# Plain 32-bit products for the cache compression of a hybrid decoder step, state scaling inside the update, and stationary keys in the prompt's compressed scores

## The chip, the cores and the metric

One Trainium2 chip, one of its cores. The metric is device time of one execution in microseconds (us), the median over runs; for the kernel before it is 1252.94 us (three runs, 1251.83 to 1259.93). TensorE multiplies, VectorE (DVE), ScalarE (ACT) and GpSimd (POOL) do the elementwise work, SyncE (SP) issues most transfers.

## The reference, cut to what matters

One layer on a prompt of 512 tokens and on 8 sample sequences of 4 new tokens with 2048 cached ones. The part that the change touches: the compression of cached keys and values (k and v alike, 8 sequences, 2 heads of 64), the compressed scores of the prompt, and the state update of the sample's mLSTM.

```python
def compress(kv, pe, w1, b1, w2):            # once for keys, once for values
    b, tk, hk, dh = kv.shape
    nc = tk // CMP_STRIDE                    # 16 rows a block
    half = CMP_STRIDE * dh                   # 1024
    ch = kv.reshape(b, nc, CMP_STRIDE, hk, dh).transpose(0, 1, 3, 2, 4).reshape(b, nc, hk, half)
    first = ch @ w1[:half]
    second = ch @ w1[half:]                  # w1: 2048 x 256
    second = jnp.concatenate([second[:, 1:], jnp.zeros_like(second[:, :1])], axis=1)
    hid = first + second + (pe.reshape(-1) @ w1 + b1)
    return jax.nn.gelu(hid) @ w2
...
        s_c = jnp.einsum('bkgqd,bkcd->bkgqc', qi, kc) - slopes * d_c     # compressed scores
...
        C_new = w_c[..., None, None] * C + jnp.einsum('bsh,bshe,bshd->bhed', w_s, vi, ki)
```

Everything is float32 in and out.

## The kernel before

The kernel is written with a tile framework whose scheduler simulates the program and so sets the order on each engine; pools of buffers and data dependencies bound it. Work runs in stages: projections and the prompt's selected and window attention (0 to about 240 us), then compression with everything else of the two attentions beside it (to 573 us), the rest of the sample's attention (to 647 us), then output projection, cross attention and feed-forward.

Dense products run as three fp32r matmuls. `split` (L213, L214) makes a high part by a ScalarE copy into fp32r and a low part by a subtraction on VectorE or GpSimd; `mm3` (L218 to L220) adds high by high, high by low and low by high into one PSUM bank.

`compress(kv)` is a generator, for keys (0) and values (1): 32 steps each, (b, t) with b one of 8 sequences and t one of 4 quarters of w1. For a step, `produce` (two steps ahead) fetches gathered pages (`cgat`, indirect transfers on GpSimd's queue, L573), transposes them with VectorE into `xf` (L1193), lets GpSimd add the two halves (L1195), and splits `xf` into `xh` and `xl` (128x768 each, L1196). Then come six products, three pairs: half one, half two and the sum of the halves by the matching weights (the last by w0 + w1, so that three products stand for four), stationary x 128x128, moving weights 128x256. For b = 0 four more with `xe`, the prompt's own blocks and the position terms (66 rows). `weights(t)` splits a quarter of w1 into `w1h` and `w1l`, adds its halves on GpSimd (L1135) and splits the sum into `wsh` and `wsl`. At t = 3 `ys` is formed (L1328 to L1330) with `nxt_`, rows shifted by a transfer from `cur` (L1300 to L1302); one sequence later it is turned (L1216), goes through gelu and the second product (L1244, L1246).

w1 for the keys is staged in two buffers of the page pool and in `vcn`, `po2` and `r3`; for the values it is loaded into a pool "w1r" once the prompt's mLSTM is done.

`weave(compress(kv), fg)` runs the compression as background and takes steps of the foreground chain for credit: 0.6 for each compression yield (three a step). The chain is `front` (the prompt's mLSTM with `cmp_prompt`, the prompt's compressed attention, mixed in), `mlstm_s` (the sample's mLSTM), `sample` (its compressed, window and selected attention in two groups of four sequences) and `open_late`. `sample` starts only when the values' weights are split (`need(("w", 1))`, L1413). In `sample` pages are gathered into `gat` (L573), turned on TensorE (`keys`, L1512), scored four sequences at a time (`quad`, L1522), normalised with exp (L1667) and multiplied by values (L1688).

`mlstm_s` turns the old state `C0` (8 sequences, 4 heads, 128x128), reads it out, scales it by `wcb` on GpSimd (L1070, two instructions of 128x2048), and adds outer products (L1100) with VectorE (`outer`, L1101, eight of 128x512).

`cmp_prompt` scores 512 prompt tokens against 32 compressed keys: for each of four token tiles eight products with the queries stationary (128x128) and 32 key columns moving (L1359), and two additions of a bias (L1362).

## Time and profile before

| | |
|---|---|
| median of three runs | 1252.94 us (1251.83 to 1259.93) |
| profiled execution | 1257.88 us |
| its span | 1256.2 us |
| busy TensorE / VectorE / ScalarE / GpSimd | 94 / 69 / 50 / 46 % |
| mean granted TensorE clock | 0.97 |
| chain that ended last | TensorE 72%, VectorE 12%, issue 5%, DMA 3%, ScalarE 3%, GpSimd 2% |
| moved | HBM read 141.67 MB, written 13.12 MB |

The profile shows one execution. A line of the trace names the engine (PE is TensorE's matmuls, PEld its weight loads), the source line, the operation and the tiles (out<-in, numbers left out). A busy engine is one with an instruction in work; matmuls are pipelined and their ends are modelled, so their spacing is read from starts. PEclk is the clock granted to TensorE as a share of full speed (2.4 GHz; the lower level is 1.2). The chain of waits follows the work that ended last back in time, from each instruction to what released it.

### The profile page before, as it was taken

How to read it: one execution, taken by the hardware profiler on the slowest of the kernel's cores; microseconds unless marked ns; L12 is line 12 of the kernel's file. 1: busy time of each engine (PE TensorE's matmuls, PEld its weight loads, DVE VectorE, ACT ScalarE, POOL GpSimd, SP SyncE). 2: the span in 40 equal slices, each digit the busy share in tenths (PEclk: the TensorE clock that was granted, in tenths of full speed). 3: DMA queues.
4: the chain of work that ended last, by engine and by line, in shares of the span. 5: the costliest groups of instructions: out<-in, count | busy, mean ns of one | idle time of the engine just before them, and what ended most of it. 6: DMA issues, size and time to landing. Idle time of an engine off the chain costs nothing.

```text
span 1256.2 us, 24868 instructions
## 1 busy us (share of the span) xinstructions
PE 1174.9 (94%) x9388; PEld 1078.2 (86%) x9388; DVE 867.2 (69%) x1881; ACT 628.6 (50%) x1424; POOL 583.9 (46%) x696
## 2 busy tenths in 40 slices
PE   7999999889998779998989998999999999999996
PEld 5998999588986677876889987589899999999996
DVE  6336674577886876776556576544988878888874
ACT  5235666755546525567533333433565555465452
POOL 1013354577664854744234100034786486486443
PEclk9999999899888899999989999999999999999998
DMA  7324240132142464567659399750023322422411
GB/s 231 100 53 105 83 151 3 52 115 76 59 133 92 124 212 147 174 208 236 160 156 179 101 217 280 258 168 1 1 92 108 104 93 79 133 93 77 135 52 72
DMA packets 141771, 154.33 MB, mean 123 GB/s; under 512 B 17449, under 2 KB 123689, under 8 KB 141394
## 3 DMA queue, kind: packets, MB, share of 16 engines
q1 hardware_dynamic: 131922, 119.17, 31.9%
q0 software_dynamic: 9728, 33.56, 8.3%
q8 instruction: 74, 1.21, 0.4%
q14 instruction: 47, 0.39, 0.1%
HBM read 141.67 MB, written 13.12 MB: 123 GB/s over the span
## 4 chain that ended last, share of the span: by engine, by line
PE 72%; DVE 12%; issue 5%; DMA 3%; ACT 3%; POOL 2%; SPq 2%; another core or an unknown queue 0%; DVEq 0%; POOLq 0%; ACTq 0%
PE bd L218 7%; PE bd L220 7%; PE xc L2255 7%; PE xa L2255 7%; PE bd L219 6%; PE bd L2255 5%; PE tp L2255 5%; PE xa L219 2%; PE xa L218 2%; PE xa L220 2%; DVE sp L2195 2%; PE tp L634 1%; PE xc L219 1%; PE xc L218 1%; PE xc L220 1%
## 5 line engine op out<-in xcount | busy, mean ns | idle before, releaser
L214 POOL TENSOR_TENSOR al<-fraw,ah 128x512 fp32r<-128x512 f32 (+1 forms) x104 | 127.3, 1226 | 152.7 <-ACT ah L213 124.2
L214 DVE TENSOR_TENSOR wlo<-wraw,whi 128x1024 fp32r<-128x1024 f32 (+3 forms) x74 | 76.4, 1061 | 27.6 <-ACT whi L213 27.4
L213 ACT ACTIVATE whi<-wraw 128x1024 fp32r<-128x1024 f32 (+3 forms) x74 | 62.9, 890 | 64.7 <-DMA wraw<-in_w_xv 28.8
L218 PE MATMUL bd<-w1h,xh 128*128 128x256 f32 x256 | 78.8, 309 | 6.6 <-ACT xh L213 5.1
L213 ACT ACTIVATE ah<-fraw 128x512 fp32r<-128x512 f32 (+1 forms) x112 | 65.8, 593 | 37.8 <-PE xc L2255 11.7
L220 PE MATMUL bd<-w1h,xl 128*128 128x256 f32 x256 | 78.7, 313 | 6.3 <-DVE xl L214 6.3
L213 ACT ACTIVATE xh<-xf 128x768 fp32r<-128x768 f32 x64 | 53.5, 842 | 52.6 <-POOL xf L1195 30.7
L1195 POOL TENSOR_TENSOR xf<-xf 128x256 f32<-128x256 f32 x64 | 52.9, 834 | 56.6 <-DVE xf L1193 38.0
L219 PE MATMUL bd<-w1l,xh 128*128 128x256 f32 x256 | 76.1, 298 | 0.0
L214 DVE TENSOR_TENSOR xl<-xf,xh 128x768 fp32r<-128x768 f32 x64 | 62.9, 987 | 15.1 <-ACT xh L213 13.7
L625 POOL TENSOR_SCALAR sb<-sb,rs,gat 128x128 f32<-128x128 f32 (+3 forms) x64 | 45.9, 722 | 54.3 <-DVE rs L624 40.2
L218 PEld LDWEIGHTS bd<-w1h,xh 128*128 128x128 f32 x256 | 51.9, 203 | 11.2 <-ACT xh L213 7.1
L213 ACT ACTIVATE ah<-sp 128x512 fp32r<-128x512 f32 (+1 forms) x64 | 35.5, 555 | 50.3 <-DVE sp L2195 26.6
L220 PEld LDWEIGHTS bd<-w1h,xl 128*128 128x128 f32 x256 | 51.2, 202 | 10.6 <-DVE xl L214 7.6
L219 PEld LDWEIGHTS bd<-w1l,xh 128*128 128x128 f32 x256 | 52.0, 203 | 1.4 <-issue 0.9
L219 PE MATMUL bd<-hlo,whi 128*128 128x272 f32 x176 | 52.0, 296 | 0.0
L218 PE MATMUL bd<-hhi,whi 128*128 128x272 f32 x176 | 51.7, 294 | 0.0
L220 PE MATMUL bd<-hhi,wlo 128*128 128x272 f32 x176 | 51.4, 292 | 0.0
L2195 DVE TENSOR_TENSOR sp<-fraw 128x512 f32<-128x512 f32 (+1 forms) x32 | 47.9, 1497 | 0.2
L214 DVE TENSOR_TENSOR al<-sp,ah 128x512 fp32r<-128x512 f32 (+1 forms) x64 | 40.8, 637 | 9.7 <-ACT ah L213 8.5
L1869 POOL TENSOR_TENSOR acc<-acc,sq 128x272 f32<-128x272 f32 x35 | 31.3, 895 | 34.3 <-ACT sq L1868 33.9
L220 PE MATMUL bd<-hh,wlo 128*128 128x272 f32 x160 | 46.6, 292 | 0.0
(998 smaller groups left out, 4830.4 us busy)
## 6 DMA issues: line engine op xcount, KB each, us to landing
fraw<-in_w_gate SPq DMA_DIRECT2D x11, 1024.0 KB
fraw<-in_w_up SPq DMA_DIRECT2D x11, 1024.0 KB
fraw<-in_w_down SPq DMA_DIRECT2D x24, 384.0 KB
mkv<-in_cache_mem_k SPq DMA_DIRECT2D x64, 128.0 KB
mkv<-in_cache_mem_v SPq DMA_DIRECT2D x16, 512.0 KB
wraw<-in_w_in SPq DMA_DIRECT2D x8, 512.0 KB
wraw<-in_w_xq SPq DMA_DIRECT2D x4, 1024.0 KB
wraw<-in_w_xk SPq DMA_DIRECT2D x4, 1024.0 KB
```

The lines of the kernel that those rows point to most:

```text
L213: nc.scalar.activation(hi, src, AF.Copy)
L214: (eng or nc.gpsimd).tensor_tensor(lo, src, hi, op=OP.subtract)
L218: nc.tensor.matmul(out, ah, bh, start=first, stop=False, **kw)
L219: nc.tensor.matmul(out, ah, bl, start=False, stop=False, **kw)
L220: nc.tensor.matmul(out, al, bh, start=False, stop=last, **kw)
L625: (nc.vector, nc.gpsimd)[1].tensor_scalar(sb[:, :n], sb[:, :n], rs, gat[:, i, 3 * h + 1 + br:3 * h + 2 + br], op0=OP.mult, op1=OP.mult)
L634: ins = nc.tensor.transpose(p[:, 128 * k:128 * k + 128], sb[:, 128 * k:128 * k + 128], ident)
L1195: nc.gpsimd.tensor_tensor(xf[:, :, 128:192], xf[:, :, 0:64], xf[:, :, 64:128], op=OP.add)
L1869: nc.gpsimd.tensor_tensor(acc[hf], acc[hf], sq, op=OP.add)
L2195: nc.vector.tensor_tensor(o, a, b, op=op)
L2255: nc.tensor.matmul(p[:, :HALF], w[a][:, k], x[b_][:, k], start=first and k == 0 and i == 0, stop=last and k == n - 1 and i == 2, skip_grou ...
```

## The change

Three parts, and what they bring along.

1. Compression multiplies plain 32-bit operands: one `mm1` takes the place of each `mm3`. The splits of x, of the weights and of `xe` go. `weights(t)` is one VectorE addition. VectorE's transpose writes `xf` in the order that the products read, in four buffers instead of two; to make that possible the gathers take rows in another order (index tables at the start of the kernel), and so do the eviction in `hidden` and the shifted rows (two transfers of 64 and 63 rows instead of 112 and 15). w1 for the keys is loaded ahead into a pool "cx"; w1 for the values into tiles of the compression's own pool; "w1r" and the wait at the start of `sample` go.
2. `mlstm_s`: the GpSimd scaling goes; the update is 32 VectorE instructions C = C * wcb + p of 128x128.
3. `cmp_prompt`: keys are stationary (128x32), the 512 queries move, four products fill one bank in strips of 32 partitions; the result is copied to SBUF (`ST`), turned per token tile by two transposes, and one addition takes the place of two.

```diff
@@ gather tables
-            nc.gpsimd.iota(psel4[:, q], pattern=[[0, 4], [1, 8], [0, 4]], base=8 * (q % 2), channel_multiplier=-1,
+            nc.gpsimd.iota(psel4[:, q], pattern=[[0, 4], [1, 16], [0, 2]], base=0, channel_multiplier=-1,
...
+        cx = push("cx", side="left")
+        w1p = {}
+        for t in range(4):
+            w1p[0, t] = cx.tile([128, 2, 2, 256], F32, name=f"w1{t}"), cx.tile([128, 2, 256], F32, name=f"ws{t}")
+            load_w1(0, t, [w1p[0, t][0][:, s] for s in range(2)])
@@ mlstm_s
-                if c == 2 or c == 4:
-                    cc = C0[c // 2 - 1]
-                    b0 = 2 * c - 4
-                    nc.gpsimd.tensor_tensor(cc, cc, wcb[:, b0:b0 + 4, :, None].to_broadcast([128, 4, 4, 128]), op=OP.mult)
...
                     nc.tensor.matmul(p, W3[:, h], kz[:, 4 * c:4 * c + 4], start=True, stop=True)
-                    nc.vector.tensor_tensor(C0[c][:, :, h], C0[c][:, :, h], p.rearrange("p (b d) -> p b d", b=4), op=OP.add)
+                    for b in range(4):
+                        x = C0[c][:, b, h]
+                        nc.vector.scalar_tensor_tensor(x, x, wcb[:, 4 * c + b, h:h + 1], p[:, 128 * b:128 * b + 128],
+                                                       op0=OP.mult, op1=OP.add)
@@ compress
-            def weights(t, raw):
-                hi, lo = [cw.tile([128, 2, 2, 256], R32, name=f"w1{c}{t}") for c in "hl"]
...
-                nc.gpsimd.tensor_tensor(raw[0], raw[0], raw[1], op=OP.add)
-                split(sh, sl, raw[0], (nc.vector, nc.gpsimd)[1])
-                w1s.append(((hi[:, 1], lo[:, 1]), (hi[:, 0], lo[:, 0]), (sh, sl)))
+            def weights(t):
+                w, ws = w1p[kv, t]
+                nc.vector.tensor_tensor(ws, w[:, 0], w[:, 1], op=OP.add)
+                w1s.append((w[:, 1], w[:, 0], ws))
+
+            def mm1(out, a, b, first, last, **kw):
+                nc.tensor.matmul(out, a, b, start=first, stop=last, **kw)
...
+                if kv == 0 and b > 0 and t == 0 and b < 5:
+                    w1p[1, b - 1] = (cw.tile([128, 2, 2, 256], F32, name=f"w1{b - 1}"),
+                                     cw.tile([128, 2, 256], F32, name=f"ws{b - 1}"))
+                    load_w1(1, b - 1, [w1p[1, b - 1][0][:, s] for s in range(2)])
...
-                xf = cw.tile([128, 4, 192], F32, name="xf", bufs=2)
-                nc.vector.transpose(xf[:, :, 0:128].rearrange("p a (q i) -> p q a i", q=4),
-                                    gs[0].rearrange("p (q t a i) -> p t q a i", q=4, t=4, a=4)[:, t])
-                nc.gpsimd.tensor_tensor(xf[:, :, 128:192], xf[:, :, 0:64], xf[:, :, 64:128], op=OP.add)
-                xh, xl = [cw.tile([128, 2, 3, 128], R32, name=f"x{c}", bufs=2) for c in "hl"]
-                split(*[x.rearrange("p c g (v j) -> p v c g j", v=2) for x in (xh, xl)],
-                      xf.rearrange("p (v c) (g j) -> p v c g j", v=2, g=3), nc.vector)
+                xf = cw.tile([128, 2, 3, 128], F32, name="xf", bufs=4)
+                nc.vector.transpose(xf[:, :, 0:2].rearrange("p c g (x v i) -> p (g x) v c i", x=2, v=2),
+                                    gs[0].rearrange("p (q t v c i) -> p t q v c i", q=4, t=4, v=2, c=2)[:, t])
+                nc.gpsimd.tensor_tensor(xf[:, :, 2], xf[:, :, 0], xf[:, :, 1], op=OP.add)
...
-                        mm3(dst[i_], (ah[:, kk], al[:, kk]), (wh[:, kk], wl[:, kk]), i_ != 1 and t == 0 and kk == 0,
+                        mm1(dst[i_], ops[i_][:, kk], w1s[t][i_][:, kk], i_ != 1 and t == 0 and kk == 0,
                             t == 3 and kk == 1, skip_group_check=True)
...
-                            mm3(px[:66, 0:256], (eh[:, kk, sl], el[:, kk, sl]), (wh[:, kk], wl[:, kk]),
+                            mm1(px[:66, 0:256], xe[:, kk, s:s + 66], w1s[t][1 - s][:, kk],
@@ cmp_prompt
+            ST = vcn.rearrange("p (v c) o -> p v (c o)", v=2)
+            for v in range(2):
+                S = bank(psp)
+                for j in range(4):
+                    nc.tensor.matmul(S[32 * j:32 * j + 32], kb[:, v], Q2[:, 4 * v + j].bitcast(F32), start=True, stop=True)
+                nc.scalar.activation(ST[:, v], S, AF.Copy)
...
-                            nc.tensor.matmul(S[:, c0:c0 + 32], Q2[:, 4 * v + j, 128 * i:128 * i + 128].bitcast(F32), kb[:, v],
-                                             start=True, stop=True)
...
+                        nc.tensor.transpose(S[:, 128 * v:128 * v + 128], ST[:, v, 128 * i:128 * i + 128], ident)
+                    nc.vector.tensor_tensor(sb, S[:, :256].rearrange("p (h s) -> p h s", h=8), CB[:, i], op=OP.add)
@@ sample
-            yield from need(("w", 1))
```

The order on TensorE where compression begins (tp, sp and po rows are the prompt's mLSTM; bd and xa are the banks of the compression, w1h, w1l, wsh the split weights and their sum, xh and xl the split input). Before:

```order
L799 MATMUL tp<-xc,wqk 128x512
L825 MATMUL sp<-qm,kmT 128x384
L802 MATMUL tp<-xc,wqk 128x32
L218 MATMUL bd<-w1h_3342,xh 128x256
L219 MATMUL bd<-w1l_3343,xh 128x256
L218 MATMUL xa<-wsh_3346,xh 128x256
L218 MATMUL bd<-w1h_3342,xeh 66x256
```

The same place of the changed kernel (w and ws are the loaded weights and their sum, xf the transposed input):

```order
L822 MATMUL sp<-qm,kmT 128x384
L796 MATMUL tp<-xc,wqk 128x512
L799 MATMUL tp<-xc,wqk 128x32
L1128 MATMUL bd<-w_3200,xf 128x256 x4
L1128 MATMUL bd<-w_3206,xf 128x256 x4
L1128 MATMUL xa<-ws_3201,xf 128x256 x2
L1128 MATMUL bd<-w_3212,xf 128x256
```

The first eight products now need loaded weights and the transposed input alone; the first that needs a sum is the ninth.

The order on TensorE at the end of compression (gat the sample's gathered pages, kt its turned keys, PTs its turned probabilities, ys and hid the compression's last output, mh and ml the input of the output projection). Before:

```order
L220 MATMUL bd<-w1h_5524,xl 128x256
L1512 MATMUL tp<-ident,gat 128x128 x12
L1216 MATMUL xc<-ident,ys 128x128 x4
L1619 MATMUL tp<-ident,pcs 127x128
L1622 MATMUL tp<-blk,GS 128x32
L1522 MATMUL sp<-kt,Qn 32x512 x4
L1512 MATMUL tp<-ident,gat 128x128 x12
L1246 MATMUL xc<-w_5414,hid 127x64 x4
L1512 MATMUL tp<-ident,gat 128x128 x12
L1522 MATMUL sp<-kt,Qn 32x512 x4
L1512 MATMUL tp<-ident,gat 128x128 x12
L218 MATMUL xa<-mh,whi 128x272
```

And in the changed kernel (L1482, L1492 and L1658 are the key transposes, scores and value products, L1364 the prompt's compressed output):

```order
L1128 MATMUL bd<-w_4135,xf 128x256 x2
L1482 MATMUL tp<-ident,gat 128x128 x8
L1189 MATMUL xc<-ident,ys 128x128 x4
L1482 MATMUL tp<-ident,gat 128x128 x4
L1492 MATMUL sp<-kt,Qn 32x512 x4
L1482 MATMUL tp<-ident,gat 128x128 x12
L1492 MATMUL sp<-kt,Qn 32x512 x4
L1219 MATMUL xc<-w_4838,hid 127x64 x4
L1364 MATMUL sp<-PcT,vcP 64x512 x2
L1189 MATMUL xc<-ident,ys 128x128 x4
L1482 MATMUL tp<-ident,SS 128x128 x4
L1364 MATMUL sp<-PcT,vcP 64x512 x2
```

Before, the pages here belong to the sample's second group, and the first group's value products stand ahead of these rows; in the changed kernel they are the first group's, and its value products follow these rows.

## Rows read from the trace of the kernel before

**Rows 1.** Page: busy time, then the span in 40 slices.
```profile
PE 1174.9 (94%) x9388; PEld 1078.2 (86%) x9388; DVE 867.2 (69%) x1881; ACT 628.6 (50%) x1424; POOL 583.9 (46%) x696
...
PE   7999999889998779998989998999999999999996
...
PEclk9999999899888899999989999999999999999998
```

**Rows 2.** Stages: length, busy us by engine, clock, DMA share, GB/s.
```profile
243.00:278.00 35.00, 28.90 (x174) 23.57 (x174) 26.44 (x47) 20.48 (x51) 28.18 (x29) 0.90 0.37 115
278.00:334.30 56.30, 54.14 (x407) 49.12 (x406) 46.29 (x107) 32.64 (x99) 40.95 (x50) 0.94 0.21 62
334.30:390.40 56.10, 52.16 (x408) 47.59 (x407) 43.43 (x103) 28.67 (x65) 31.00 (x37) 0.89 0.40 123
390.40:440.50 50.10, 38.52 (x289) 32.31 (x288) 38.59 (x56) 26.60 (x58) 35.34 (x28) 0.85 0.34 100
440.50:500.90 60.40, 50.60 (x428) 44.51 (x427) 41.48 (x116) 23.41 (x51) 31.87 (x42) 0.94 0.54 182
500.90:572.90 72.00, 71.35 (x663) 58.37 (x662) 50.51 (x106) 45.14 (x81) 41.87 (x46) 1.00 0.63 198
572.90:647.20 74.30, 63.85 (x575) 54.47 (x573) 44.89 (x103) 39.87 (x85) 21.39 (x27) 0.93 0.61 184
```

**Rows 3.** TensorE timeline, fp32r products: start us, us, line.
```profile
406.88 0.28 PE L218 MATMUL xa<-wsh,xh 128*128 128x256 f32 x1
...
408.06 0.28 PE L219 MATMUL bd<-w1l,xh 128*128 128x256 f32 x1
```

**Rows 4.** 32-bit scores of the cross attention: timeline, then line L2136.
```profile
778.13 1.03 PE L2136 MATMUL xc<-KTm,qx 128*128 128x256 f32 x4
...
L2136 PE MATMUL xc<-KTm,qx x32: 379/379/483, 778.1 to 816.7; 128*128 128x256 f32 x32
```

**Rows 5.** TensorE timeline: prompt's scores, sample's scores, transposes.
```profile
348.54 1.87 PE L1359 MATMUL sp<-kb,Q 128*128 128x32 f32 x16
...
511.64 1.07 PE L1522 MATMUL sp<-kt,Qn 128*32 128x512 f32 x8
...
514.58 1.04 PE L1512 MATMUL tp<-ident,gat 128*128 128x128 f32 x8
```

**Rows 6.** Groups of 240 to 575 us: xcount | busy, mean ns | idle.
```profile
L214 DVE TENSOR_TENSOR xl<-xf,xh 128x768 fp32r<-128x768 f32 x64 | 62.9, 987 | 15.1 <-ACT xh L213 13.7 <-issue 0.6 <-PE xa L220 0.6
...
L213 ACT ACTIVATE xh<-xf 128x768 fp32r<-128x768 f32 x64 | 53.5, 842 | 52.6 <-POOL xf L1195 30.7 <-PE xa L219 9.8 <-PE bd L219 6.2
...
L1195 POOL TENSOR_TENSOR xf<-xf 128x256 f32<-128x256 f32 x64 | 52.9, 834 | 56.6 <-DVE xf L1193 38.0 <-DVE ksT L210 4.9 <-ACT xh L213 3.8
...
L1193 DVE STREAM_TRANSPOSE xf<-cgat 128x512 f32<-128x512 f32 x64 | 44.6, 701 | 2.2 <-DMA cgat<-in_cache_k_cmp,gx 1.7
```

**Rows 7.** Chain of waits by line, 243-573 us, then 243-260 us.
```profile
by line: issue 10.0%; PE bd L218 8.4%; PE bd L220 8.4%; PE bd L219 7.6%; PE tp L1512 3.7%; PE xa L219 3.4%; PE xa L218 3.2%; PE xa L220 3.2%; DVE xl L214 3.1%; DMA gat<-in_state_v_win 2.9%; PE tp L832 2.7%; DVE w1l L214 2.6%; PE sp L1522 2.
...
by line: issue 19.6%; POOL cgat L1135 13.0%; POOL A L818 9.7%; PE bd L218 8.3%; POOL vcn L1135 7.3%; DVE w1l L214 7.3%; PE bd L219 5.7%; ACT xh L213 5.0%; PE bd L220 4.5%; POOL xf L1195 4.2%; PE po L811 3.0%; POOL po L1135 2.8%; PE sp L825 
```

**Rows 8.** Chain of waits by line, 390-440 us.
```profile
by line: DVE w1l L214 14.9%; DMA nxt<-cur 10.4%; DVE xl L214 9.0%; issue 8.0%; DVE dns L1078 7.0%; PE bd L220 6.3%; PE bd L218 5.2%; DVE C L1101 5.1%; PE bd L219 4.8%; DVE hid L1234 3.3%; PE tp L1100 2.9%; DVE xf L1193 2.7%; DVE hs L1086 2.
```

**Rows 9.** Four lines: ns min/median/max, first and last start us.
```profile
L1070 POOL TENSOR_TENSOR C<-C,wcb x2: 3609/4106/4603, 395.1 to 411.3; 128x2048 f32<-128x2048 f32 x2
...
L1101 DVE TENSOR_TENSOR C<-C,tp x8: 643/681/690, 409.2 to 425.8; 128x512 f32<-128x512 f32 x8
...
L1362 DVE TENSOR_TENSOR csb<-sp,CB x8: 267/279/291, 315.4 to 356.0; 128x128 f32<-128x128 f32 x8
...
L1093 DVE SCALAR_TENSOR_TENSOR nsn<-n,wN,sp x4: 327/331/334, 385.8 to 399.7; 8x128 f32<-8x128 f32 x4
```

**Rows 10.** Waits of 243-640 us: us in total, times, longest.
```profile
POOL gat L573 <- PE tp L1512: 22.0, 7, 12.4
```

**Rows 11.** TensorE timeline at 562 us.
```profile
562.44 1.08 PE L1688 MATMUL po<-gat,PTs 128*32 128x128 f32 x32
```

More of the change, by code (lines that the diff above doesn't have):

```diff
@@ L557, in body @@
         nc.vector.tensor_scalar(ri[:, 2], ri[:, 2], 5, None, op0=OP.logical_shift_right)
-        nc.vector.tensor_scalar(ri[:, 1], ri[:, 0], 3, None, op0=OP.bitwise_and)
-        nc.vector.tensor_scalar(ri[:, 1], ri[:, 1], 8, None, op0=OP.mult)
+        nc.vector.tensor_scalar(ri[:, 1], ri[:, 0], 1, None, op0=OP.bitwise_and)
+        nc.vector.tensor_scalar(ri[:, 1], ri[:, 1], 16, None, op0=OP.mult)
         nc.vector.tensor_tensor(ri[:, 3], ri[:, 1], ri[:, 2], op=OP.add)
-        nc.vector.tensor_scalar(ri[:, 4], ri[:, 3], 4, None, op0=OP.add)
+        for q in range(1, 4):
+            nc.vector.tensor_scalar(ri[:, 3 + q], ri[:, 3], 4 * (q // 2) + 8 * (q % 2), None, op0=OP.add)
         p = bank(ptp)
@@ L565, in body @@
         nc.vector.tensor_tensor(gx[:, 0], p[:, :8], ri[:, 0], op=OP.add)
-        nc.vector.tensor_tensor(gx[:, 3:7].rearrange("p (g x) b -> p g x b", g=2),
-                                p[:, 8:40].rearrange("p (g x b) -> p g x b", g=2, x=2),
-                                ri[:, 3:5, None].to_broadcast([128, 2, 2, 8]), op=OP.add)
+        nc.vector.tensor_tensor(gx[:, 3:7], p[:, 8:40].rearrange("p (q b) -> p q b", q=4), ri[:, 3:7], op=OP.add)
         for h in range(2):
@@ L588, in load_w1 @@
                     nc.sync.dma_start(dst[s_][:, c], w1[t, c, s_])
-        def stage_w1():
-            cgs["w"] = cgp.tile([128, 2, 2, 2, 256], F32, name="cgat", bufs=2)
-            for t in range(2):
-                load_w1(0, t, [cgs["w"][:, t, s] for s in range(2)])
         pop("wp")
@@ L1124, in compress @@
             w1s = []
[L1126 to L1149 removed]
+            def weights(t):
[4 more added lines that the diff above has]
+                nc.tensor.matmul(out, a, b, start=first, stop=last, **kw)
+            weights(0)
             w2 = cw.tile([128, 2, 64], F32, name="w2")
@@ L1183, in produce @@
                 if b == 0 and t > 0:
-                    weights(t, raws[t])
-                if kv == 0 and b > 0 and "w" not in cgs and "ml" not in right and "mlstm" in done:
-                    wp_ = push("w1r", side="left")
-                    cgs["w"] = wp_.tile([128, 2, 2, 2, 256], F32, name="wr")
-                    prompt_cols(1, r3, wp_.tile([128, 512], F32, name="pp"))
-                    for u in range(4):
-                        load_w1(1, u, [cgs["w"][:, u, s] for s in range(2)] if u < 2 else
-                                ([vr[:, s] for s in range(2)], pr_)[u - 2])
@@ L1199, in produce @@
-                if b == 0:
-                    hi, lo = [cw.tile([128, 2, 68], R32, name=f"xe{c}") for c in "hl"]
-                    split(hi[:, :, 64:68], lo[:, :, 64:68], peT[:, 2 * t:2 * t + 2, 0:4], nc.vector)
-                    h_, l_ = [x[:, :, 0:64].rearrange("p c (v i) -> p v c i", v=2) for x in (hi, lo)]
-                    split(h_, l_, cgs["p", kv].rearrange("p (t v c i) -> p t v c i", t=4, v=2, c=2)[:, t], nc.vector)
-                    st["e", t] = hi, lo
-                if b == 0 and t == 3:
-                    if kv == 1:
-                        pop("w1r")
-                    done.add(("w", kv))
@@ L1209, in produce @@
-                st[b, t] = [(xh[:, :, g], xl[:, :, g]) for g in range(3)]
+                    weights(t)
+                if kv == 0 and b > 0 and t == 0 and b < 5:
+                    w1p[1, b - 1] = (cw.tile([128, 2, 2, 256], F32, name=f"w1{b - 1}"),
+                                     cw.tile([128, 2, 256], F32, name=f"ws{b - 1}"))
+                    load_w1(1, b - 1, [w1p[1, b - 1][0][:, s] for s in range(2)])
+                    if b == 4:
+                        prompt_cols(1, r3, cw.tile([128, 512], F32, name="pp"))
@@ L1211, in turned @@
+                st[b, t] = [xf[:, :, g] for g in range(3)]
             def turned(src, n, m):
@@ L1222, in hidden @@
                     if n == 2:
-                        nc.scalar.activation(hx[:, hb].rearrange("p (v j g) -> p g v j", v=2, g=2),
-                                             p[:, 256 * hb:256 * hb + 256].rearrange("p (g v j) -> p g v j", g=2, v=2),
+                        nc.scalar.activation(hx[:, hb].rearrange("p (v i x g) -> p g x v i", v=2, x=2, g=2),
+                                             p[:, 256 * hb:256 * hb + 256].rearrange("p (g x v i) -> p g x v i", g=2, x=2, v=2),
                                              AF.Identity, bias=bia[:, hb:hb + 1])
@@ L1811, in body @@
         weave(compress(0), fg)
-        if "w" not in cgs:
-            raise RuntimeError("w1r")
         late.pop()()
```

46 lines of the change are left out of this document (12 added, 34 removed).

## The prediction

> **What bounds the kernel now.** I read the page first, then the table by stage, then the chain of waits inside single stages, and last the timeline of TensorE for prices. The page [rows 1] shows a kernel that TensorE bounds: it is busy 94% of the span, VectorE 69%, ScalarE 50%, GpSimd 46%. Two dents stand in its line of forty slices (31.4 us each): the 8th and 9th (220 to 283 us) and the 13th to 15th (377 to 471 us); the granted clock falls to eight tenths in the 8th and from the 11th to the 14th (314 to 440 us). The table by stage [rows 2] puts numbers on the part that the change touches, the compression of the paged cache (243 to 572.9 us) and what stands behind it until the residual norm's sums (647.2 us). Over the six compression rows TensorE is busy 295.7 of 329.9 us, so 34.2 us are idle; and the granted clock there is 0.90, 0.94, 0.89, 0.85, 0.94 and 1.00, so that busy time times (1 - clock) is another 2.9 + 3.2 + 5.7 + 5.8 + 3.0 + 0 = 20.6 us that a full clock would not need. TensorE thus loses about 55 us in compression, nearly all before 501 us: the last row (500.9 to 572.9) is full, 71.35 of 72.0 at clock 1.00. The reader is to see both halves in this: in the first 258 us others hold TensorE up and there is something to win, in the last 72 nothing does and every added TensorE cycle is paid.
>
> **The products.** One product of the compression is now three fp32r matmuls; at full clock they start 0.118 us apart (406.88 to 408.06 us: ten steps in 1.18 us [rows 3]), 0.354 us for the three. The plain 32-bit product leaves two records for one instruction; the same form, 128x128 stationary and 128x256 moving, runs in the cross attention: four records take 1.03 us and the record of one is 0.379 [rows 4], so they start (1.03 - 0.379) / 3 = 0.217 us apart, and a product takes 0.434. That is 0.080 us more. There are 6 products in each of 64 steps and 32 for the prompt's rows, 416 in all: **+33.3 us** of TensorE. At the lowest mean clock of a stage, 0.85 [rows 2], the same difference is 33.3 / 0.85 = +39, the end above; a product cheaper than this row is rival C.
>
> The Trainium skill, "FP8 and Floating Point Precision" (TensorE Precision Notes), says that true 32-bit products are four passes of the array, and reduced precision reads one: by that rule a product would be 4 x 0.118 = 0.472 against 0.354, an estimate of +49 us, with which the sum below would be +16.6 and the time 1269.5. The row gives 0.434, which is four passes of 0.108: the trace agrees in kind, and the row's number is used. The rule speaks against this change.
>
> **The prompt's scores.** Sixteen records of 32 columns take 1.87 us with the tail of the last [rows 5]; I take 1.7, four times: 6.8 us. After it two sets of four 512-column products in 32-column strips, the form of the sample's scores (1.07 us a set [rows 5]), and 8 transposes of two records each; eight such records take 1.04 us with the tail of the last [rows 5], so I take 0.11 a record, 1.8 us: 3.9 in all. **-2.9 us**. Two evictions to SBUF on ScalarE (half idle) come in, and four additions go.
>
> **The splits.** Each of 64 steps loses a ScalarE copy of 842 ns and a VectorE subtraction of 987 ns, together 53.5 and 62.9 us, and keeps VectorE's transpose (701 ns) and GpSimd's addition (834 ns) [rows 6]. The weights' splits go too, and VectorE takes over their sum (8 additions of 128x512; nearest row 0.68 us [rows 9], so 5.4 us, hidden beside TensorE once the first is done). What this is worth is read from the chain of waits, since most of it lies beside TensorE. Over 243 to 573 us [rows 7] the subtractions are 3.1% (xl) and 2.6% (w1l) of the chain: 10.2 + 8.6 = 18.8 us. At the start, 243 to 260 us, GpSimd's sums of the weights (L1135) are 13.0 + 7.3 + 2.8% and the first xh 5.0%: 28.1% of 17 = 4.8 us, and there I count the whole, because after the change the first eight products need the loaded weights and a transpose alone, and the ninth is the first to need a sum. In 390 to 440 us [rows 8] w1l and xl are 23.9% of 50 = 12.0 us, inside the 18.8; the ScalarE copies between them (wsh, w1h, xh), which the row does not print, I put at 2.4, about a fifth of it. Sum **-26 us** (bounds: 0, if what is behind each split is just as late, and -34, all idle time). What is late next is the transpose and GpSimd's addition, 1.5 us for 2.6 us of products, with four buffers instead of two: not the bound.
>
> **State scaling.** GpSimd's two passes over the state (3.6 and 4.6 us) go; 8 VectorE additions of 0.68 become 32 fused ones of 128x128 [rows 9]. No row has that form: the nearest are 0.279 (128x128 from PSUM, no scalar) and 0.331 (fused, but 8 partitions): 8.9 to 10.6 us against 5.4, so +3.5 to +5.2 of VectorE; I take the fused one, +5. Queued behind them stand the transposes of compression and the state's read-out, and the outer products wait for the bank that they read: L1101 is 5.1% of the chain of that stretch, 2.6 us [rows 8]; doubled, **+3 us** on the path (bounds 0 and +5). GpSimd's 8.2 us are no gain of their own: it waits there anyway.
>
> **Clock.** In the two stages from 334 to 440 us TensorE ran at 0.89 and 0.85, after idle pieces. With the splits gone I take 0.95 for 278 to 440 us: 0.05 x 144.8 = 7.2 us lost instead of 14.7, **-7.5 us** (bounds 0 and -15).
>
> **Work that moves behind.** TensorE's order shows that the sample's selected attention now stands later: behind the last compression product there are 88 key transposes instead of 60 (two records each), 16 more of the scores, 64 more value products, three more sets of scores and the prompt's last compressed output. By the rows: 44 x 0.22 [rows 5] + 4 x 1.0 (16 value products, 32 records, in 1.08 [rows 11]) + 3 x 1.07 + about 4 (my estimate for the prompt's output) = 21 us of work that leaves the compression stretch and stands in the 74.3 us behind. That is no loss where TensorE is as full; it is 0.86 there (63.85 of 74.3) against 0.90 in compression [rows 2]: 21 / 0.86 - 21 / 0.90 = **+1 us** (bounds 0 and +19, rival B).
>
> **Sum.** +33.3 - 2.9 - 26 + 3 - 7.5 + 1 = **+0.9 us** on the profiled execution (1257.88; span 1256.2), which is 0.4% above the median of 1252.94. I add it to the median: **1253.8 us**. Against the rest of the kernel (up to 243 us and from 647 us on) the change does nothing that TensorE's order or a price shows.
>
> **Rivals.**
> A, the stalls go altogether. TensorE then runs through compression as in 501 to 573 us, where it is full at clock 1.00 [rows 2]. Of the 55 us lost 8 remain (start and the state's read-out): -47 + 30.4 + 1 = -15.6, **1237 us**. For it: two of the four vector-engine steps in front of each step's products go. Against it: in 390 to 440 us the transfer of the shifted rows (10.4%) and the read-out's vector work (dns 7.0%) are on the chain and stay [rows 8].
>
> B, the sample's attention runs uncovered. Before, the first group's last value products ended at 563.5 us [rows 11], still under compression, and the residual norm's sums came at 647.2, the end of the last stage [rows 2]: 84 us of a chain of gather, transpose, score, exponential and value. After the change the first group's values all stand behind the last compression product, with some 19 us of TensorE rows in front of and among them, so that the chain ends 19 + 84 = 103 us behind that product instead of 74.3; 21 us of the 29 have left compression, +8. The second group's gathers write the buffers which those values and transposes read: GpSimd already waits 22.0 us for them, 12.4 at the longest [rows 10], under cover of compression. Uncovered that is +12: together 8 + 12 - 1 (the term it replaces) on top of +0.9 gives +20, **1273 us**. It decides when the stretch from the last compression product to the norm passes 105 us. Against it: the output projection's products fill part of that stretch in both orders.
>
> C, a plain product takes the time of two fp32r ones, 2 x 0.1185 = 0.237 us: (0.237 - 0.354) x 416 = -48.7 instead of +33.3, some **1172 us**. The row of the same form [rows 4], 0.434, speaks against it. The Trainium skill, "Perfetto Trace Analysis" (Engine Utilization), divides TensorE's peak by two for 32-bit low/high products; by that rule C would come out, and the trace does not agree.
>
> **How the numbers follow.** Forecast 0.46, A 0.25, B 0.27, C 0.02. A measurement of this kernel can tell about 1% (12.5 us) from no change. The forecast's own range, with the half of its bounds that I find likely (splits -30 to -18, clock -11 to -4), is 1245 to 1264; with A and B it is 1232 to 1275, which leaves out C and the far ends. Faster by over 1%: most of A, C, a little of the forecast, 0.28; slower: most of B and a little of the forecast, 0.28; within 1%: 0.44.
>
> **What would show it.** Right: plain products 0.43 us apart at full clock; first compression product near 250 us; the chain of 390 to 440 us without splits; TensorE full from about 290 us on; compression over at 550 to 560 us and the stretch behind it near 100 us. Wrong: a product under 0.38 or over 0.48 us at full clock; granted clock in 278 to 440 us still under 0.90 (clock term); a stretch behind compression over 105 us (B) or under 85 (the order moved nothing); the chain of 390 to 440 us led by the fused state updates (the +3).

## The result, and the profile after

The changed kernel takes **1273.03 us** (median of four, 1270.72 to 1275.58) against 1254.63 us of the kernel before beside it: ratio **1.0135**, 95% interval 1.010 to 1.017. In a second group of runs it was 1.0197 (1.0161 to 1.0234). It is slower by over 1%, inside the range given (1232 to 1275), but not the likeliest case (no change, 1253.8): it lies where rival B was put (1273). The profiled execution took 1273.35 us, span 1271.6, so a span 15.4 us longer than before.

The page of the changed kernel (busy time; the span in 40 slices, now 31.8 us each) answers to [rows 1]:

```profile
PE 1195.0 (94%) x8932; PEld 1069.2 (84%) x8932; DVE 787.8 (62%) x1821; ACT 577.1 (45%) x1344; POOL 541.2 (43%) x678
...
PE   7998999578999999997899998999999999999996
...
PEclk9998999689999999997889999999999999999998
```

VectorE is 79 us less busy, ScalarE 52, GpSimd 43, and TensorE 20 more. The dent at the 13th to 15th slice is gone; the 8th has become deeper, and a new one stands at the 19th and 20th slice. The table by stage of the changed kernel (length, busy us of each engine, clock, DMA share, GB/s) answers to [rows 2]:

```profile
217.00:243.00 26.00, 17.62 (x123) 13.50 (x122) 8.85 (x36) 11.60 (x37) 7.83 (x15) 0.80 0.24 82
243.00:264.00 21.00, 14.53 (x91) 9.67 (x89) 7.43 (x18) 8.54 (x20) 5.46 (x14) 0.76 0.08 22
264.00:300.00 36.00, 24.82 (x106) 18.24 (x105) 10.58 (x23) 5.60 (x21) 8.24 (x11) 0.91 0.33 107
300.00:350.00 50.00, 50.00 (x273) 41.33 (x273) 24.36 (x68) 20.74 (x69) 29.13 (x41) 1.00 0.25 71
...
500.00:554.80 54.80, 54.80 (x367) 44.32 (x366) 25.82 (x70) 16.73 (x34) 25.99 (x32) 1.00 0.56 171
554.80:610.00 55.20, 46.25 (x368) 30.99 (x367) 28.94 (x63) 36.36 (x65) 21.03 (x24) 0.88 0.64 208
610.00:663.60 53.60, 47.81 (x442) 41.20 (x439) 27.38 (x70) 24.21 (x56) 12.11 (x15) 0.87 0.51 149
```

Five times set against those of the kernel before tell where the 16 us at the residual norm come from:

| | before | after | difference |
|---|---|---|---|
| mLSTM's first projection on TensorE | 239.3 | 255.9 | +16.6 |
| first product of the compression | 255.6 | 264.0 | +8.4 |
| last product of its first sequence | 278.0 | 300.0 | +22.0 |
| last product of all | 572.9 | 554.8 | -18.1 |
| residual norm's sums | 647.2 | 663.6 | +16.4 |

So the start loses 22 us, the other fifteen sequences win 40 (294.9 us before, 254.8 after, TensorE full from 300 us on), and the stretch behind the last product grows by 34.5 us, from 74.3 to 108.8. The reader should take the first line with the last: the foreground chain, which starts with the mLSTM, takes 407.9 us before and 407.7 after. In these two profiles it only starts later. The equality is a balance and no constant: the same stretch takes 393.7 us with the new state update alone (e5 below) and 420.8 with the plain products alone (e11).

What makes it start late, the chain of waits from 225 to 300 us shows (its summary, and its pieces on loads and sums: start us, us, what):

```profile
by line: SPq L587 31.9%; DMA w<-in_cmp_w_v 11.3%; DMA w<-in_cmp_w_k 10.8%; PE bd L1128 8.5%; PE xc L640 7.3%; PE tp L796 6.2%; PE tp L628 2.9%; PE sp L822 2.4%; SPq L778 2.3%; PE xa L1128 2.3%; ACT A L814 2.2%; issue 1.9%; DVE ws L1124 1.8%
...
236.45 8.13 DMA w<-in_cmp_w_k
...
244.71 0.69 DVE ws L1124
...
281.28 1.30 SPq L778
...
284.73 8.46 DMA w<-in_cmp_w_v
...
293.38 0.69 DVE ws L1124
```

More than half of these 75 us are the loads of w1: 31.9% their issue on SyncE (L587), 22.1% their way. Between SyncE's 13th and 14th load of the values' w1 stands a load of the mLSTM's projection weights (L778, 281.28 us), which the scheduler had put there. The kernel before issued eight of the keys' sixteen loads at 22 us (the first row); in the changed kernel all sixteen come in one row at 219.6 to 236.4 us (the second). So for half of the keys' w1 the pool "cx" is no earlier place but a later one:

```profile
L588 SPq DMA_DIRECT2D cgat<-in_cmp_w_k x8: 523/660/1459, 22.2 to 28.2; - x8
...
L587 SPq DMA_DIRECT2D w<-in_cmp_w_k x16: 528/1226/2032, 219.6 to 236.4; - x16
```

The waits of the same stretch (us in total, times, longest) name who stood there:

```profile
DVE ws L1124 <- DMA w<-in_cmp_w_v: 21.9, 4, 7.5
...
DVE ws L1124 <- DMA w<-in_cmp_w_k: 13.3, 4, 4.7
```

VectorE waited 35.2 us at the head of its queue for weights whose sums it was to make, while the softmax rows of the prompt's selected attention (before 264 us) and the mLSTM's steps stood behind. The order showed these eight additions where the wait occurs; the prediction gave them 0.7 us each and looked at no wait.

The prices of the products and the update came out as read. A timeline row of the changed kernel at full clock, and line L1096 (ns min/median/max):

```profile
313.77 1.03 PE L1128 MATMUL bd<-w,xf 128*128 128x256 f32 x4
```

```profile
L1096 DVE SCALAR_TENSOR_TENSOR C<-C,wcb,tp x32: 306/340/348, 447.3 to 467.7; 128x128 f32<-128x128 f32 x32
```

Four records in 1.03 us are the row of [rows 4] over again, 0.434 us a product; an update takes 0.340, close above the upper of the two bounds.

### The profile page after: what moved, and what is told of

Read it like the earlier page. It is cut to its first block, busy times and chain, and to the rows that moved or that the text cites. A ratio compares the mean times of both kernels' runs of the same rounds, so it can differ in the third digit from the quotient of the medians.

```text
span 1271.6 us, 23742 instructions
## 1 busy us (share of the span) xinstructions
PE 1195.0 (94%) x8932; PEld 1069.2 (84%) x8932; DVE 787.8 (62%) x1821; ACT 577.1 (45%) x1344; POOL 541.2 (43%) x678
## 4 chain that ended last, share of the span: by engine, by line
PE 77%; DVE 7%; DMA 5%; SPq 4%; ACT 3%; issue 2%; POOL 1%; another core or an unknown queue 0%; POOLq 0%; DVEq 0%; ACTq 0%
PE bd L1128 9%; PE xc L2224 7%; PE xa L2224 7%; PE bd L2224 5%; PE tp L2224 5%; PE bd L219 4%; PE bd L218 4%; PE bd L220 4%; PE xa L1128 4%; SPq L587 2%; PE tp L1482 2%; PE xa L218 2%; PE xa L219 2%; PE xa L220 2%; PE xc L219 1%
## 5 line engine op out<-in xcount | busy, mean ns | idle before, releaser
L1128 PE MATMUL bd<-w,xf 128*128 128x256 f32 x512 | 126.9, 386 | 0.0
L1128 PEld LDWEIGHTS bd<-w,xf 128*128 128x128 f32 x512 | 95.4, 193 | 14.2 <-issue 1.8
L619 POOL TENSOR_SCALAR sb<-sb,rs,gat 128x128 f32<-128x128 f32 (+3 forms) x64 | 43.2, 680 | 76.6 <-DVE rs L618 69.2
L1128 PE MATMUL xa<-ws,xf 128*128 128x256 f32 x256 | 64.8, 383 | 0.6 <-DVE ys L1298 0.6
L1173 DVE STREAM_TRANSPOSE xf<-cgat 128x512 f32<-128x512 f32 x64 | 44.0, 700 | 16.8 <-PE xa L1128 9.4
L1128 PEld LDWEIGHTS xa<-ws,xf 128*128 128x128 f32 x256 | 46.4, 190 | 8.1 <-issue 2.9
L617 ACT ACTIVATE sb<-sb,mn 128x128 f32<-128x128 f32 (+3 forms) x64 | 35.6, 557 | 24.7 <-DVE mn L615 24.3
L218 PE MATMUL bd<-hh,whi 128*128 128x272 f32 x160 | 46.4, 290 | 0.0
L219 PE MATMUL bd<-hl,whi 128*128 128x272 f32 x160 | 46.3, 289 | 0.0
L213 ACT ACTIVATE ah<-po 128x512 fp32r<-128x512 f32 (+1 forms) x64 | 35.7, 557 | 22.7 <-PE xa L2224 14.0
```

What stands on the lines that cost most here:

```text
L213: nc.scalar.activation(hi, src, AF.Copy)
L218: nc.tensor.matmul(out, ah, bh, start=first, stop=False, **kw)
L219: nc.tensor.matmul(out, ah, bl, start=False, stop=False, **kw)
L617: nc.scalar.activation(sb[:, :n], sb[:, :n], AF.Exp, scale=-1.0, bias=mn, accum_out=rs)
L619: (nc.vector, nc.gpsimd)[1].tensor_scalar(sb[:, :n], sb[:, :n], rs, gat[:, i, 3 * h + 1 + br:3 * h + 2 + br], op0=OP.mult, op1=OP.mult)
L1128: nc.tensor.matmul(out, a, b, start=first, stop=last, **kw)
```

## The experiments

Theory H, formed on the rows above: the sums at the head of VectorE's queue, and behind them the loads, hold the start, and that is the loss. Theory K: TensorE's 33 us of dearer products are the loss, and an earlier start is given back later. The ratio is to the kernel before, run beside them in three groups (e1 to e4; e0, e5, e6 and e8; e9 to e12). The one profile of the kernel before is of an execution of 1257.88 us, while its medians in these groups are 1248.5, 1249.0 and 1255.3; so a difference between a profile and that one can be off by up to 9 us, and the ratios decide.

| run | what it is | ratio | 95% interval |
|---|---|---|---|
| e0_changed | the changed kernel again | 1.0197 | 1.0161 to 1.0234 |
| e1_keys | keys' sums later on VectorE | 1.0170 | 1.0142 to 1.0197 |
| e2_values | values' sums later on VectorE | 1.0237 | 1.0212 to 1.0261 |
| e3_both | both | 1.0189 | 1.0159 to 1.0220 |
| e4_loads | both, and values' loads later on SyncE | 1.0074 | 1.0049 to 1.0100 |
| e8_late | as e4, and half the keys' loads later | 1.0033 | 1.0004 to 1.0063 |
| e9_noscores | as e8, old scores | 1.0079 | 1.0048 to 1.0111 |
| e11_products | as e8, old scores, old state update | 1.0159 | 1.0130 to 1.0188 |
| e10_pace | as e8, sample's steps at 0.5 | 0.9999 | 0.9979 to 1.0018 |
| e12_mix | as e9, sample's steps at 0.5 | 1.0121 | 1.0093 to 1.0150 |
| e5_state | kernel before, new state update | 0.9923 | 0.9894 to 0.9951 |
| e6_scores | kernel before, new scores | 1.0101 | 1.0065 to 1.0137 |

The changed kernel once more, beside e5, e6 and e8:

> The changed kernel again, on the chip of the other three runs of this group, so that these can be compared with it: 1.0135 times the kernel before within its interval of 1.010 to 1.017.

Its 1.0197 is above the first measurement's 1.0135; the intervals overlap from 1.0161 to 1.017. Both are used below.

### The sums' place on VectorE

```diff
-            weights(0)
...
-                if b == 0 and t > 0:
-                    weights(t)
...
-                nc.vector.transpose(xf[:, :, 0:2]...
+                turn = nc.vector.transpose(xf[:, :, 0:2]...
+                if b == 0:                      # e1: and kv == 0; e2: and kv == 1
+                    with tc.issue_after(turn.ins):
+                        weights(t)
```

Keys alone:

> The changed kernel with the four weight sums of the keys queued on VectorE behind the transposes of the same step instead of among the prompt's softmax rows. Theory H (the sums stand at the head of VectorE's queue and wait there for w1's transfers, and the foreground chain starts late): the mLSTM's first projection comes back from 255.9 us to 241 to 246, and 8 to 14 us of that reach the end: 1259 to 1265 us. The values' sums still hold VectorE near 270 to 290 us. Theory K (416 products dearer by 0.08 us are the whole loss): an earlier start is given back later, 1270 to 1274 us.

Values alone:

> The changed kernel with only the four sums of the values' weights moved back behind the transposes of the values' first sequence. Theory H: the first sequence of the keys takes 24 to 28 us instead of 36 and the wait of 21.9 us on VectorE for the values' w1 goes; start stays at 255.9; 1255 to 1265 us. Theory K: 1270 to 1274 us.

Both:

> Both sets of sums moved. Theory H: the gains add, 1240 to 1252 us, at or below the kernel before. Theory K: 1268 to 1274 us, since the work on TensorE is what it was.

The keys' sums moved, the mLSTM's first projection comes at 242.7 us instead of 255.9, and the first sequence ends at 288.6 instead of 300.0: as H said of the start. But the time does not follow: 1.0170, 1.0237 and 1.0189 are not below the 1.0197 of the changed kernel by more than their intervals. H as stated falls. All three also lie above what K expected (1.011 to 1.015 by 1254.63 us). In e1 the earlier start is given back: the residual norm's sums come at 656.7 us, against 663.6 and 659.3 in the two profiles of the changed kernel. With the values' sums out of the way the first sequence still takes to 299.2 us (e2) and 293.3 (e3), so something else stands behind them.

### The loads on SyncE

```diff
-                if kv == 0 and b > 0 and t == 0 and b < 5:
+                if kv == 0 and b > 1 and t == 0 and b < 6:
...
-                    load_w1(1, b - 1, ...)
+                    with tc.issue_after(moved[-1].ins):      # the last transfer of shifted rows
+                        load_w1(1, b - 2, ...)
...
```

> As the run with both sets of sums moved, and the values' w1 is loaded one sequence later each, behind the transfers of the shifted rows, so that the mLSTM's projection weights do not stand behind 16 of these loads on SyncE's queue. If the queue of loads held the mLSTM too, 3 to 8 us less than the run with both sums moved; if only VectorE's queue mattered, the same within 2 us.

1.0189 becomes 1.0074, 15.9 us by the medians where 3 to 8 were expected, and the intervals lie apart. The issue rows of the loads show the difference. Both sums moved (e3; ns min/median/max, first and last start us):

```profile
L778 SPq DMA_DIRECT2D wqk<-in_w_qm x4: 329/784/2103, 237.7 to 299.3; - x4
```

```profile
L587 SPq DMA_DIRECT2D w<-in_cmp_w_v x16: 528/1267/4440, 252.5 to 275.8; - x16
```

And with the values' loads held back (e4, lines L778 and L587 of that kernel):

```profile
L778 SPq DMA_DIRECT2D wqk<-in_w_qm x4: 328/352/1192, 238.1 to 283.5; - x4
```

```profile
L587 SPq DMA_DIRECT2D w<-in_cmp_w_v x16: 528/542/608, 275.6 to 331.6; - x16
```

Sixteen loads close together took SyncE 1.27 us each at the median and 4.44 at the worst; in four rows of four they take 0.54. The mLSTM's last projection weights are issued at 283.5 us instead of 299.3 (before: 275.0), and the first sequence of the compression ends at 278.2 instead of 293.3. The same treatment for half the keys' loads:

```diff
-            load_w1(0, t, ...)
+            if t < 2:
+                load_w1(0, t, ...)
...
+        with tc.issue_after(qk[1].ins):          # the mLSTM's first projection weights
+            for t in range(2, 4):
+                load_w1(0, t, ...)
```

> The run with sums and values' loads held back, and in addition the third and fourth quarter of the keys' w1 are loaded behind the mLSTM's first projection weights. If SyncE's queue in front of these weights is what keeps the mLSTM's start at 244.9 us there (before: 239.3), the start comes back to 238 to 241 us and the time falls by another 3 to 6 us, to a ratio of 1.002 to 1.005; if something else holds the start, the ratio stays at 1.0074.

The first projection comes at 239.4 us (before 239.3) and the ratio is 1.0033, as expected. Two reserves belong to it: its interval overlaps that of e4, and e9 to e12 below, whose order on TensorE is the same as here up to 324 us, start the mLSTM at 241.5 to 243.2 us, so that a part of these 5.5 us is one execution's.

From 1.0197 to 1.0033, 19 us by the medians, is thus the price of how w1 arrives, on two queues; against the first measurement of the changed kernel, 1.0135, it is 13 us. Moving the sums on VectorE's queue alone gained nothing that the intervals show. Loads held back with the sums left in their place were not tried, so how much of it is VectorE's queue stays open.

### The three parts by themselves

e5 is the kernel before with this:

```diff
-                    nc.gpsimd.tensor_tensor(cc, cc, wcb[:, b0:b0 + 4, :, None].to_broadcast([128, 4, 4, 128]), op=OP.mult)
...
-                    nc.vector.tensor_tensor(C0[c][:, :, h], C0[c][:, :, h], p.rearrange("p (b d) -> p b d", b=4), op=OP.add)
+                        nc.vector.scalar_tensor_tensor(x, x, wcb[:, 4 * c + b, h:h + 1], p[:, 128 * b:128 * b + 128],
+                                                       op0=OP.mult, op1=OP.add)
```

e6 is the kernel before with this:

```diff
+            ST = vcn.rearrange("p (v c) o -> p v (c o)", v=2)
...
+                    nc.tensor.matmul(S[32 * j:32 * j + 32], kb[:, v], Q2[:, 4 * v + j].bitcast(F32), start=True, stop=True)
+                nc.scalar.activation(ST[:, v], S, AF.Copy)
...
-                            nc.tensor.matmul(S[:, c0:c0 + 32], Q2[:, 4 * v + j, 128 * i:128 * i + 128].bitcast(F32), kb[:, v],
-                                             start=True, stop=True)
...
+                        nc.tensor.transpose(S[:, 128 * v:128 * v + 128], ST[:, v, 128 * i:128 * i + 128], ident)
...
```

e9 takes the second of these edits out of e8, and e11 both. What was expected of e5, e6, e9 and e11, in this order:

> The kernel before with the state update alone changed (no GpSimd scaling, 32 fused VectorE instructions). By the prediction's term, +3 us (0 to +5), ratio 1.000 to 1.004. The rival is that the removed GpSimd passes (8.2 us) stood in the way of the compression's additions: then -3 to -8 us, 0.994 to 0.998.

> The kernel before with the prompt's compressed scores alone changed (keys stationary). By the prediction's term, -2.9 us if TensorE bounds that stretch, ratio 0.997 to 0.999; the rival is that the foreground chain there waits for vector work and transfers, so that nothing comes of it: 1.000 within 0.002.

> The run with sums, values' loads and half of the keys' loads held back (ratio 1.0033), with the prompt's compressed scores as before the change. If stationary keys cost by the order that they bring to the foreground chain, in any kernel, the ratio falls by the 0.010 that they added to the kernel before: 0.990 to 0.997. If they cost there only because their copy lies where the values' weights were staged, which the changed kernel does not do, the ratio stays at 1.000 to 1.006.

> Plain products with the held-back sums and loads, and neither the new state update nor the new scores. If the 33 us of added products are paid by the splits' stalls, as in the prediction's sum, 0.996 to 1.006. If TensorE's work is the bound (theory K), 1.010 to 1.024.

The state update wins 0.8% in both places: 0.9923 on the kernel before, and 1.0159 to 1.0079 between e11 and e9. On the kernel before that is a little more than the rival's 0.994 to 0.998. Timeline rows of GpSimd and VectorE of the kernel before show one thing that the removed passes did:

```profile
395.11 3.61 POOL L1070 TENSOR_TENSOR C<-C,wcb 128x2048 f32<-128x2048 f32 x1 [5.26 <-PE tp L1058]
...
411.34 4.60 POOL L1070 TENSOR_TENSOR C<-C,wcb 128x2048 f32<-128x2048 f32 x1
```

```profile
396.55 3.25 DVE L214 TENSOR_TENSOR w1l<-wr,w1h 128x1024 fp32r<-128x1024 f32 x1
...
412.40 3.56 DVE L1078 TENSOR_TENSOR dns<-dns 128x1 f32<-128x1 f32 x1
```

And the same two VectorE steps in e5, where these passes are gone, with the GpSimd addition that stands beside the second (GpSimd is idle beside the first):

```profile
394.23 1.21 DVE L214 TENSOR_TENSOR w1l<-wr,w1h 128x1024 fp32r<-128x1024 f32 x1
...
408.01 0.71 DVE L1074 TENSOR_TENSOR dns<-dns 128x1 f32<-128x1 f32 x1
...
407.55 1.15 POOL L1194 TENSOR_TENSOR xf<-xf 128x256 f32<-128x256 f32 x1
```

A maximum of one column took 3.56 us beside a GpSimd pass of 4.60 and ended with it (415.96 and 415.94 us); in e5 it took 0.71 and ended with a shorter GpSimd addition (408.72 and 408.70). Both VectorE steps stood on the chain of waits in that stage ([rows 8]: w1l 14.9%, dns 7.0%). So the rival's number came, but by slower VectorE steps, where it had named GpSimd's additions. These two steps alone are 2.0 + 2.9 = 4.9 us shorter, about what the fused updates add (32 x 0.34 = 10.9 against 5.4 us); the larger part of the 9.6 us won comes from what followed in that stage and behind it (sequence 9 ends at 429.5 us instead of 440.5), and that I did not take apart. The Trainium skill, "SBUF — State Buffer" (SBUF: two separate sides), states that VectorE and GpSimd share one pair of ports as an exclusive lock: of a VectorE instruction with two inputs in SBUF and a GpSimd one, whichever starts first keeps it for its whole length, and the other is blocked. These rows agree: both VectorE steps have two such inputs, began after the GpSimd pass (395.11 and 411.34 us) and ended with it or 1.08 us, about a w1l's own 1.21, behind it.

The scores are not settled. On the kernel before they cost +1.0%, outside both cases expected of e6. In the changed kernel e8 with them is 0.5% below e9 without (1.0033 and 1.0079), but the intervals overlap, and 3.2 us of the difference are there at the mLSTM's first projection (239.4 and 242.6 us), before the first instruction that the two order differently on TensorE; e9 lies above both cases expected of it. In e6 the copy of the scores lies in `vcn`, where a part of the values' weights was staged, so those loads moved from 251.5 to 346.0 us, and the ones into `wr` from 376.4 to 383.7. Its chain from 390 to 440 us:

```profile
by line: DMA wr<-in_cmp_w_v 23.5%; DVE CT L1054 9.5%; DMA w<-in_cmp_w_v 7.3%; DVE w1l L214 4.6%; ACT kz L1108 4.4%; issue 4.3%; DMA nxt<-cur 4.3%; PE tp L1100 3.9%; DVE w L1152 3.8%; DMA hidt<-in_cmp_b_v 3.3%; PE bd L218 2.2%; SPq L1158 2.2
...
389.80 11.76 DMA wr<-in_cmp_w_v
```

The 11.76 us there are a wait for the values' weights in `wr`. But that does not account for e6's loss: its compression is over at 566.8 us, 6.1 earlier than before, and its whole span (1257.7 us) is only 1.5 longer than that of the kernel before, whose profiled execution was slower than its medians. Where the 1.0% go stays open, and no run prices the scores: e6 also moves loads, and e8 against e9 (some 6 us by the ratios) is within its uncertainty.

e11 prices the products, together with what they bring along (order of the gathers, buffers, shifted rows, w1's new places): 1.0159. With the loads mended but for 3.8 us of the mLSTM's start (243.1 against 239.3), plain products in place of splits still cost 20 us, what K expected (1.010 to 1.024) and not the 0.996 to 1.006 of the prediction's sum. The page of e11 shows it for the whole span (before: [rows 1]):

```profile
PE 1206.4 (95%) x8972; PEld 1077.7 (85%) x8972; DVE 790.0 (62%) x1801; ACT 575.8 (45%) x1342; POOL 545.9 (43%) x680
```

TensorE is busy 31.5 us longer than before (1206.4 against 1174.9), nearly the 33 us of the dearer products, and idle only 13.2 us less (68.1 of 1274.5 against 81.3 of 1256.2). Where that comes about is the next question.

### Where the compression's gain goes

The table by stage of e8 (columns as above):

```profile
250.00:300.00 50.00, 50.00 (x247) 39.38 (x246) 23.57 (x60) 16.94 (x58) 21.46 (x28) 1.00 0.34 102
300.00:350.00 50.00, 49.91 (x302) 41.22 (x301) 31.48 (x68) 20.77 (x67) 35.52 (x46) 1.00 0.31 91
350.00:400.00 50.00, 50.00 (x310) 41.89 (x309) 35.42 (x94) 22.47 (x57) 29.83 (x38) 0.99 0.42 121
400.00:440.00 40.00, 38.43 (x252) 27.65 (x251) 22.26 (x88) 12.20 (x39) 12.91 (x24) 0.93 0.35 102
440.00:526.60 86.60, 86.51 (x548) 71.46 (x547) 44.79 (x122) 28.81 (x56) 45.59 (x54) 1.00 0.65 206
526.60:644.20 117.60, 93.31 (x799) 69.99 (x797) 54.71 (x131) 59.68 (x119) 32.77 (x39) 0.87 0.53 161
```

TensorE is full for some 275 us at a clock of 0.93 to 1.00, and compression is over at 526.6 us, 46 us earlier than before. Rival A's picture has come true for this stretch. But the stretch behind it is 117.6 us instead of 74.3, with TensorE busy 93.3 of them at a clock of 0.87: 43 of the 46 us are back. From the sample's first key transposes to the norm it now takes 203 us (441.2 to 644.2), before 185 (462.2 to 647.2). e11 has the same picture:

```profile
440.00:547.10 107.10, 104.77 (x665) 84.59 (x663) 49.14 (x129) 32.61 (x66) 51.71 (x61) 0.98 0.55 178
547.10:663.90 116.80, 93.25 (x760) 69.53 (x759) 52.50 (x126) 57.42 (x116) 30.86 (x35) 0.82 0.51 151
```

Does TensorE's order stretch the sample's attention?

```diff
-        fg = chain(paced(front(), 1.3), paced(mlstm_s(), 2), paced(sample(), .8), open_late())
+        fg = chain(paced(front(), 1.3), paced(mlstm_s(), 2), paced(sample(), .5), open_late())
```

Expected of e10, then of e12:

> The same run with the new scores kept and a step of the sample's attention priced at 0.5 instead of 0.8 in the weaving, so that more of it is laid among the compression's products and less behind them (72 key transposes and five sets of scores behind the last product instead of 80 and six). If the stretch from the sample's first key transposes to the norm (203 us, before 185) is long because TensorE's order puts too many products among its rows, it shortens to 190 to 197 us and the ratio falls to 0.994 to 1.000; if it waits for gathers and vector work, the ratio stays within 0.003 of 1.0033.

> Plain products with held-back sums and loads, the new state update, the old scores, and the sample's steps priced at 0.5. If the single effects add, 0.985 to 0.994, below the kernel before; if TensorE's work or the gathers bound it, 0.997 to 1.005.

It is not settled by this. e10 has the ratio expected of the order (0.9999), but the stretch in question is 203.7 us in its profile, not 190 to 197, and the intervals of e10 and e8 overlap, so its 0.9999 may be no gain at all. e12 is a miss: 1.0121, outside both cases and no faster than its like without the new pace (e9, 1.0079; the intervals overlap). The chain of waits behind compression in e8 points elsewhere (526 to 645 us, and its three longest pieces):

```profile
by line: DMA wraw<-in_w_out 24.1%; PE po L1666 9.3%; issue 6.0%; PE tp L1490 4.8%; ACT kt L206 3.5%; PE sp L1372 3.5%; ACT whi L213 3.4%; DVE wlo L214 3.1%; PE sp L1500 2.8%; PE tp L1381 2.5%; POOL hl L214 2.3%; ACT mh L213 2.1%; ACT SS L16
...
571.41 13.99 DMA wraw<-in_w_out
...
590.58 7.29 DMA wraw<-in_w_out
...
623.07 7.37 DMA wraw<-in_w_out
```

A quarter of it, 29 us, waits for the output projection's weights; in e11 the same row stands at 18.4% of 118 us, 22 us, and in the kernel before at 12.0% of 74, 9 us. In e11 the stretch grew by 42.5 us: TensorE is busy 29.4 us longer in it (93.25 against 63.85) and idle 13.1 longer, about what the wait for these weights grew by. Of the 29.4, by busy time times clock (93.25 x 0.82 against 63.85 x 0.93), I estimate 17 as work that moved there and 12 as the lower granted clock. All this is read from chains and tables, and an earlier load of these weights was not tried. In the changed kernel itself the same row is 7.1% of 109 us, 8 us, no more than before.

No version with plain products beats the kernel before. The kernel before with the new state update alone does: 1239.9 us, ratio 0.9923 (0.9894 to 0.9951).

## Why the prediction was right and wrong, by its own steps

**Right in its range, wrong in its likeliest case.** What was right: the prices of the product (0.434), the fused update (0.340 against bounds of 0.279 and 0.331), compression over at 550 to 560 us (554.8), and rival B's time and point of decision: the stretch behind passed 105 us (108.8), the first group's values ended 24.8 us behind the last product (19 were counted), and from there to the norm it took 84.0 us (84). The first compression product, put near 250 us, came at 264.0.

**The step that failed** is in "The splits": the 8 sums of the weights at 5.4 us, "hidden beside TensorE once the first is done", and with it the -4.8 us at the start, which became +16.6 for the foreground and +22 for the first sequence. The sum priced the additions and not the wait for their inputs: VectorE stood 35.2 us at these eight, and the loads that it waited for held SyncE's queue as well; half of the keys' had been issued some 200 us earlier in the kernel before. e0 to e4 and e8 put the arrival of w1 at 19 us (13 by the first measurement), and with it mended the ratio is 1.0033, +4 us, near the sum's +0.9.

**But that the rest of the sum came near is luck: its terms are wrong both ways.** The state update was put at +3 and is -9.6: "GpSimd's 8.2 us are no gain of their own" left out that VectorE was slowed beside those passes. The scores were put at -2.9; e8 against e9 gives about -6, within its uncertainty. The products, the splits and the clock were right together, though no run takes them apart: for compression itself the terms give 33.3 - 26 - 7.5 - 21 / 0.90 = -23.5 us, and in e11 it ends 25.8 us earlier (547.1 us). Mis-sized is "Work that moves behind", +1: the stretch behind compression, put at 21 / 0.86 = +24.4 us, grew by 42.5 (116.8 us), 18 us more, at the end of the bound of +19 that was kept for rival B. The 21 itself is misread: a 128x128 transpose leaves one record in the trace and not two (160 key transposes of the sample leave 160, L1512), so 44 of them are 44 x 0.11 = 4.8 us and the sum 16; likewise the scores' 8 transposes are 0.9 us instead of 1.8, and their term -3.8. As bookkeeping, with one profile's 18 us and the uncertain -3 of the scores, the sum by measured terms is +0.9 + 19 + 18 - 12.6 - 3 = +22, between the two measurements of the changed kernel (+17 and +25).

**The rivals.** B had the place right, the sample's attention uncovered behind compression: there e11 lost its 18 us. The mechanism that it named is not shown. GpSimd did wait longer there for the page buffers (16.5 us before, 33.5 in the changed kernel), but the chain puts e11's waiting on the output projection's weights. That B's 1273 us met the measured 1273.03 is luck as well: the changed kernel's time also held the late w1, and e8, with a longer stretch behind (117.6 us against 108.8), is 20 us faster. A came true inside compression (full TensorE, clock 1.00), but the norm gained only 3.0 us of the 46 (e8). It counted dns among what stays; without the GpSimd passes it fell to 0.71 us. C is out by the product's row.

## What to carry to other kernels

Price an added instruction by what it waits for and what is queued behind it on its engine, and follow its inputs onto the issuing queue too: here moving it on one queue gained nothing until the loads were moved on the other. Before crediting removed stalls, ask for the chain that runs beside the relieved stretch (here from the mLSTM to the norm, 394 to 421 us by kernel): what it still needs comes behind, uncovered. When one part of a bundle wins and others lose, measure each alone in both kernels: the state update won 0.8% in both, while the scores' loss of 1.0% in the one did not show in the other.

## What the runs showed of the hardware that I had not expected

A VectorE maximum of one column took 3.56 us beside a GpSimd pass over 128x2048 and ended with it; in e5, without that pass, it took 0.71 and ended with a shorter GpSimd addition.

SyncE needed 0.54 us to issue a load of w1 in rows of four (e4), but 1.27 us at the median, 4.44 at the longest, when sixteen came close together (e3). In the changed kernel's row for the keys the first five took 3.02 us (0.60 each) and the other eleven 15.49 (1.41 each); the kernel before's row of eight at 22 us also slows at the sixth (0.52 to 0.70 us each, then 1.27 to 1.46). What SyncE waits for there, the trace doesn't show.
